# RWKV inverse on 64x64 pieces, with keys prepared at full height and decayed queries on GpSimd

## The chip, the cores and the metric

The kernel runs on one core of a Trainium2 chip. A core has five engines that run beside one another, each through its own queue in order: TensorE (PE in the profile, its weight loads PEld), VectorE (DVE), ScalarE (ACT), GpSimd (POOL) and SyncE (SP, which issues the transfers here). The metric is the device time of one execution, in microseconds (us), as the median of several runs.

## The reference, cut to what matters

The program is a backbone of two layers over 256 context tokens and 1,024 latent tokens, 1,024 wide. Layer 0 runs an RWKV-7 branch (8 heads of 64 columns) beside a Mamba-2 branch; layer 1 runs an mLSTM branch beside attention. Only the RWKV branch is touched. Per head and direction the reference scans the tokens with a 64x64 state S:

```python
kk = hs(k * p['k_k'])
kk = kk / jnp.maximum(jnp.sqrt(jnp.sum(kk * kk, -1, keepdims=True)), 1e-12)
k_dir = k[:, :, None] * (1.0 + (a - 1.0) * p['k_a'])
y, S_fin = rwkv7_bidir_scan(hs(r), hs(k_dir), hs(v), hs(decay), hs(a), kk, S0)
```

At each token the state is decayed per key column, loses what it holds along kk (weighted by a), and gains the outer product of value and key; the output is the state applied to r.

## The kernel before, in words

**The stage.** RWKV runs as a stage of its own in layer 0. The 512 columns make four column tiles (ct) of 128 partitions, two heads in each: head h lies on partitions H[h], 0 to 63 or 64 to 127. Tokens are cut into chunks of 64. A unit (`rwkv_unit`) takes NG = 2 chunks of both directions, that is NJ = 4 blocks j, for both heads; a column tile has 10 units, so there are 40. Two streams run side by side: stream 0 has column tiles 0 and 1, stream 1 has 2 and 3. In a stream the unit q+1 is prepared while the chain (`rwkv_chain`) of unit q carries the state, one step of the chain to two of the unit (`pace`). Beside them go, by `rwkv_stream`, the preparation of the next column tile (`rwkv_prep`) and the closing of the last (`rwkv_finish`), and at the start the output projection of the other branch (tile `oa`).

**What a unit does.** It loads r, k, kk and the low-rank inputs, and forms the gate a and the decay (lines 685 to 711). Lines 713 to 720 prepare: AR holds, for each block, the decayed kk (slot 0) and the decayed queries (slot 1), 128 partitions high. KB holds for each block the two keys divided by the decay, the removal key P*a and the gain key P*kd, in two slots whose order differs between the heads, so four half-height products write it. RZ holds the decayed queries of each head with zeros in the other head's rows. Then matmuls of KB against AR give all products of a chunk (line 727); they are masked into MN (line 730).

**The inverse.** Within a chunk the removals depend on one another, which is a triangular 64x64 system; its inverse is built by doubling in lines 740 to 780. MT and TT are 128x128 for each block: head 0's 64x64 in one corner, head 1's in the other, and zeros elsewhere (set once, lines 578 and 582). Line 752 makes the start, TT = MT times the mask m1. Then for b = 2 to 32 a matmul px (MT against Tm), a masked copy Xs, a matmul pz (TT against Xs) copied to Tm, and a matmul pt (Xs against TT) that ScalarE copies back to the two corners of TT (line 779). The helper `halves` issues each of these as eight matmuls, over blocks and heads. Each contracts over all 128 rows, takes one head's 64 columns, and writes that head's 64 partitions.

**The chain.** For each of the two chunks: pw, copied with a minus sign to w; pu, which is TT against w (line 817); pS, the new state; py, the output. In pw, pS and py the operands MN, KT and RZ hold both heads over all 128 rows.

**What sets the order.** The queues of this stage aren't written out by hand: a planner orders the instructions of each engine from their dependencies and its own estimates of time, and puts the semaphores. A matmul has no line of its own in the profile: all are recorded at line 212 of the helper `mm`, transposes at line 215, so they are told apart by their tiles (out<-moving,stationary). Tiles `rec` are those of the unit, `ch` those of the chain.

Of the kernel before, what the change touches and what calls it, by code (L numbers as in the profile page):

```python
# [8 lines left out]
F32 = mybir.dt.float32  # L9
# [3 lines left out]
ALU = mybir.AluOpType  # L13
# [11 lines left out]
NG = 2  # L25
# [22 lines left out]
def _masks():  # L48
    parts = []
    o = 0  # L50

    def put(name, a):
        nonlocal o
        a = np.asarray(a, np.float32).reshape(128, -1)
        _MK[name] = (o, a.shape[1])
        parts.append(a)
        o += a.shape[1]

    put("id", np.eye(128))
    put("ones", np.ones((128, 128)))  # L60
    r = np.arange(128)
    hh = (r[:, None] // 64 == r[None, :] // 64)
    put("bd1", hh)
    put("triu", r[:, None] <= r[None, :])
    put("slt", r[:, None] < r[None, :])
    for d in range(2):
        ok = (r[:, None] <= r[None, :]) if d == 0 else (r[:, None] >= r[None, :])
        put(f"mb{d}", np.where(ok, 0.0, -1e30))
    put("end", np.zeros((128, 0)))
    i = r % 64  # L70
    mp, m1, lv = [], [], {b: [] for b in (1, 2, 4, 8, 16, 32)}
    for d in range(2):
        bef = (i[:, None] < np.arange(64)[None]) if d == 0 else (i[:, None] > np.arange(64)[None])
        inc = bef | (i[:, None] == np.arange(64)[None])
        beffull = (i[:, None] < i[None, :]) if d == 0 else (i[:, None] > i[None, :])
        mp += [np.concatenate([bef, inc], 1)] * NG
        m1.append((hh & beffull & (i[:, None] // 2 == i[None] // 2)) | np.eye(128, dtype=bool))
        for b in lv:
            c = np.arange(64)[None]
            lv[b].append(~inc & (i[:, None] // (2 * b) == c // (2 * b)) & (i[:, None] // b != c // b) | (i[:, None] == c))  # L80
    put("mP", np.concatenate(mp, 1))
    put("m1", np.concatenate(m1, 1))
    put("id2", i[:, None] == np.arange(64)[None])
    for b in lv:
        put(f"l{b}", np.concatenate(lv[b], 1))
    return np.ascontiguousarray(np.concatenate(parts, 1))
# [64 lines left out]
class K:  # L151
# [401 lines left out]
    def rwkv_setup(s, rp):  # L553
        nc = s.nc
        s.rp = rp
        s.mk2 = rp.tile([128, MASKS.shape[1] - NMK], F32, name="mk2")
        s.load(s.mk2, s.I["masks"][:, NMK:])
        s.w2 = rp.tile([128, 512], F32, name="w2")
        s.a2 = rp.tile([128, 512], F32, name="a2")
        s.load(s.w2, s.I["w2"])  # L560
        s.load(s.a2, s.I["a2"])
        s.smask = rp.tile([128, 2, NG, 64], F32, name="smask")
        nc.vector.memset(s.smask, 1.0)
        for d in range(2):
            nc.vector.memset(s.smask[:, d, :, 63 * d:63 * d + 1], 0.0)
        s.rc = rp.tile([128, 28], F32, name="rc")
        nc.vector.tensor_scalar_mul(s.rc[:, 0:16], s.p("w0", 0, 16), 0.5)
        ka = s.p("k_a", 0, 4)
        nc.vector.tensor_scalar_mul(s.rc[:, 16:20], ka, 0.5)
        nc.vector.tensor_scalar(s.rc[:, 20:24], ka, -0.5, 1.0, ALU.mult, ALU.add)  # L570
        nc.vector.tensor_scalar(s.rc[:, 24:28], ka, -1.0, 2.0, ALU.mult, ALU.add)
        s.tt, s.wa, s.rz, s.mt = {}, {}, {}, {}
        for st in range(2):
            for i in range(2):
                s.tt[st, i] = rp.tile([128, 2 * NG, 128], F32, name=f"TT{st}{i}")
                s.wa[st, i] = rp.tile([128, 2, 2, 64 * NG], F32, name=f"wa{st}{i}")
                s.rz[st, i] = rp.tile([128, 2 * NG, 2, 64], F32, name=f"RZ{st}{i}")
                nc.gpsimd.memset(s.tt[st, i], 0.0)
                nc.gpsimd.memset(s.wa[st, i], 0.0)
                nc.gpsimd.memset(s.rz[st, i], 0.0)  # L580
            s.mt[st] = rp.tile([128, 2 * NG, 128], F32, name=f"MT{st}")
            nc.gpsimd.memset(s.mt[st], 0.0)
        s.RX = {}
        s.tn = [0, 0]
        s.kk_d = [s.dram("kkd", (128, NT)) for _ in range(4)]
        s.bv_d = [s.dram("bvd", (128, NT)) for _ in range(4)]
        s.vt_d = [s.dram("vtd", (128, 20, 64)) for _ in range(4)]
# [60 lines left out]
    def rwkv_unit(s, st, ct, gi):  # L648

        nc, rp = s.nc, s.rp  # L650
# [6 lines left out]
        H = [slice(0, 64), slice(64, 128)]  # L657

        def tl(nm, w, bufs=1):
            return rp.tile([128, NJ] + list(w), F32, tag=f"{nm}{st}", name=s.name(nm), bufs=bufs)  # L660
# [4 lines left out]
        def rec(*sh):  # L665
            return s.psum(f"rec{st}", (128, NJ) + sh)

        r, k, kk = tl("ur", [64]), tl("uk", [64]), tl("ukk", [64])
# [3 lines left out]
        TT, RZ, MT = s.tt[st, par], s.rz[st, par], s.mt[st]  # L672
# [15 lines left out]
        sg, a = tl("sg", [64]), tl("a", [64])  # L688
        for j, x in ((0, sg), (1, a)):
            for d in range(2):  # L690
                b = 8 * j + 4 * d + ct
                nc.scalar.activation(flat(x)[:, L * d:L * d + L], pp[:, j, d], AF.Tanh, bias=s.rc[:, b:b + 1], scale=0.5)
        yield
        kd = tl("kd", [64])
        nc.vector.tensor_scalar(sg, sg, 0.5, 0.5, ALU.mult, ALU.add)
        nc.vector.tensor_scalar(kd, a, s.rc[:, 16 + ct:17 + ct], s.rc[:, 20 + ct:21 + ct], ALU.mult, ALU.add)
        nc.vector.tensor_scalar(a, a, 0.5, 0.5, ALU.mult, ALU.add)
        P = tl("P", [64])
        for d in range(2):
            def v(x):  # L700
# [4 lines left out]
        E2 = tl("E2", [64], 2)  # L705
# [1 line left out]
        nc.scalar.activation(E2, P, AF.Exp, scale=-DEC)  # L707
        nc.scalar.activation(P, P, AF.Exp, scale=DEC)
        nc.scalar.activation(sg, sg, AF.Exp, scale=-DEC)
        nc.gpsimd.tensor_mul(a, kk, a)  # L710
        nc.gpsimd.tensor_mul(kd, kd, k)
        yield
        AR = tl("AR", [2, 64])
        nc.vector.tensor_mul(AR[:, :, 0], sg, kk)
        nc.vector.tensor_mul(AR[:, :, 1], E2, r)
        KB = tl("KB", [2, 64])
        for h in range(2):
            nc.vector.tensor_mul(KB[H[h], :, h], P[H[h]], a[H[h]])
            nc.vector.tensor_mul(KB[H[h], :, 1 - h], P[H[h]], kd[H[h]])
            nc.gpsimd.tensor_mul(RZ[H[h], :, h], E2[H[h]], r[H[h]])  # L720
        yield
        MN = tl("MN", [2, 2, 64], 2)
        mP = s.m("mP").rearrange("p (j a b) -> p j a b", a=2, b=64)
        pa = [rec(2, 64) for h in range(2)]
        for j in range(NJ):
            for h in range(2):
                s.mm(pa[h][:, j].rearrange("p a b -> p (a b)"), KB[H[h], j].rearrange("p a b -> p (a b)"),
                     AR[H[h], j].rearrange("p a b -> p (a b)"))
        for h in range(2):
            nc.vector.tensor_mul(MN[:, :, :, h], pa[h], mP)  # L730
# [8 lines left out]

        ident = s.m("id")  # L740
        for h in range(2):
            nc.vector.scalar_tensor_tensor(MT[H[h], :, H[h]], MN[H[h], :, 0, h], -1.0,
                                           ident[H[h], H[h]].unsqueeze(1).to_broadcast([64, NJ, 64]), ALU.mult, ALU.add)
        KT = tl("KT", [2, 64], 2)
        pk = [rec(64) for h in range(2)]
        for j in range(NJ):
            for h in range(2):
                s.tr(pk[h][:, j], KB[H[h], j].rearrange("p a b -> p (a b)"), ident[H[h], H[h]])
        for h in range(2):
            nc.scalar.copy(KT[:, :, h], pk[h])  # L750
            nc.scalar.copy(MN[H[h], :, 0, h], AR[H[h], :, 0])
# [3 lines left out]
        def halves(fn):  # L755
            for j in range(NJ):
                for h in range(2):
                    fn(j, H[h])

        Tm = tl("Tm", [64], 2)  # L760
        px = rec(64)
        halves(lambda j, Q: s.mm(px[Q, j], MT[:, j, Q], s.m("id2")))
        nc.vector.tensor_mul(dj(Tm), dj(px), bj("l1"))  # L763
        yield
        for b in (2, 4, 8, 16, 32):
            px = rec(64)
            halves(lambda j, Q: s.mm(px[Q, j], MT[:, j, Q], Tm[:, j]))
            Xs = tl("Xs", [64])
            nc.vector.tensor_mul(dj(Xs), dj(px), bj(f"l{b}"))
            yield  # L770
            if b < 32:
                pz = rec(64)
                halves(lambda j, Q: s.mm(pz[Q, j], TT[:, j, Q], Xs[:, j]))
                Tm = tl("Tm", [64], 2)
                nc.scalar.copy(Tm, pz)
            pt = rec(64)
            halves(lambda j, Q: s.mm(pt[Q, j], Xs[:, j], TT[:, j, Q]))
            for h in range(2):
                nc.scalar.copy(TT[H[h], :, H[h]], pt[H[h]])  # L779
            yield  # L780
        X["u", gi] = {"E2": E2, "MN": MN, "KT": KT, "SV": SV, "TT": TT, "RZ": RZ}

    def rwkv_chain(s, st, ct, gi):
        nc, rp = s.nc, s.rp
        X = s.RX[ct]
        H = [slice(0, 64), slice(64, 128)]
        U = X["u", gi]
        SV, TT, MN, KT, E2, RZ = (U[k] for k in ("SV", "TT", "MN", "KT", "E2", "RZ"))
# [11 lines left out]
        def ch():  # L800
            return s.psum(f"ch{st}", (128, 2, 64))

        E = E2.rearrange("p j l -> p (j l)")
        ident = s.m("id")
        for n in range(NG):
# [5 lines left out]
            w = rp.tile([128, 2, 64], F32, tag=f"w{st}", name=s.name("w"))  # L811
            nc.scalar.mul(w, pw, -1.0)
            yield
            pu = ch()
            for d, j in enumerate(js):
                for h in range(2):
                    s.mm(pu[H[h], d], TT[:, j, H[h]], w[:, d])
            nc.vector.tensor_copy(both(SV, n)[H[0], :, 1, 0], pu[H[0]])
            nc.scalar.copy(both(SV, n)[H[1], :, 1, 1], pu[H[1]])
            yield  # L820
# [1226 lines left out]
```

## Time and profile before

| | |
|---|---|
| median of 3 runs | 3814.51 us (3805.86 to 3820.41) |
| the profiled execution | 3798.59 us |
| its span, first to last instruction | 3796.8 us |
| busy: PE | 3400.6 us (90%) |
| busy: DVE | 2253.9 us (59%) |
| busy: ACT | 1575.3 us (41%) |
| busy: POOL | 1087.7 us (29%) |
| mean granted clock of TensorE | 0.934 |
| first and last matmul of the inverse (tile rec) | 978.7 and 1882.4 us |

How to read it: times of rows are busy times of one profiled execution. A matmul's end is modelled and matmuls overlap, so PE's busy time is more than what it needs; the time from start to start tells more. In a group row stand the line, engine, operation, out<-in by the program's names, partitions x elements, the count, then the sum of busy time, the mean of one in ns, and the idle time before with what ended it. "128*64" on a matmul means 128 rows by 64 columns of the array.

### The profile page before, as it was taken

The numbers are of one execution on the slowest core, as the hardware profiler recorded it, in microseconds if no ns is written. First come the engines' busy times: TensorE is split into PE (matmuls) and PEld (weight loads), VectorE is DVE, ScalarE is ACT, GpSimd is POOL, SyncE is SP. The second block draws the span as 40 slices with busy tenths as digits, with TensorE's granted clock in tenths as the row PEclk, the third lists the DMA queues.
The fourth block names the chain that finished last, engine by engine and source line by source line (L and its number), as shares of the span: only waits on it lengthen the run. The fifth ranks groups of instructions, "written<-read, shape, count | busy, mean of one in ns | idle before, by whom it ended". The sixth has DMA issues, their size and how long they took to land. (4 is left out here: it accounts for less than half of the span.)

```text
span 3796.8 us, 74389 instructions
## 1 busy us (share of the span) xinstructions
PE 3400.6 (90%) x29178; PEld 2723.1 (72%) x29178; DVE 2253.9 (59%) x4173; ACT 1575.3 (41%) x3419; POOL 1087.7 (29%) x1037
## 2 busy tenths in 40 slices
PE   7999998886898898789869899999999788999978
PEld 3687876673577777677757798788888566666757
DVE  3576587773566667677557705433444488677645
ACT  3232233333535656555533322322232225666751
POOL 0112266553322221121102212112222255444330
PEclk9999998997899988799879999999999899999989
DMA  6526454436543222221132322654554451000023
GB/s 237 180 75 199 138 173 149 156 124 182 153 124 99 63 69 65 82 56 47 32 111 100 124 91 85 190 180 138 161 160 147 146 157 54 23 23 22 19 81 111
DMA packets 394278, 429.65 MB, mean 113 GB/s; under 512 B 81376, under 2 KB 317760, under 8 KB 391368
## 3 DMA queue, kind: packets, MB, share of 16 engines
q1 hardware_dynamic: 393928, 424.90, 35.7%
q8 instruction: 230, 3.77, 0.4%
q14 instruction: 120, 0.98, 0.1%
HBM read 306.69 MB, written 118.05 MB: 112 GB/s over the span
## 5 line engine op out<-in xcount | busy, mean ns | idle before, releaser
L212 PE MATMUL mm<-hh,wh 128*128 128x512 f32 (+1 forms) x1640 | 634.8, 387 | 0.0
L212 PE MATMUL mm<-hh,wl 128*128 128x512 f32 (+1 forms) x1640 | 610.4, 372 | 0.9 <-POOL wl L359 0.9
L212 PE MATMUL mm<-hl,wh 128*128 128x512 f32 (+1 forms) x1640 | 610.6, 372 | 0.0
L359 POOL TENSOR_TENSOR wl<-wr,wh 128x1024 fp32r<-128x1024 f32 x99 | 248.3, 2512 | 543.1 <-ACT wh L358 520.9
L212 PEld LDWEIGHTS mm<-hh,wh 128*128 128x128 f32 x1640 | 315.0, 192 | 67.8 <-issue 12.7
L212 PEld LDWEIGHTS mm<-hl,wh 128*128 128x128 f32 x1640 | 314.6, 192 | 61.4 <-issue 10.6
L212 PEld LDWEIGHTS mm<-hh,wl 128*128 128x128 f32 x1640 | 313.9, 191 | 59.5 <-issue 3.4
L1792 POOL TENSOR_SCALAR aP<-aP,adn,one 128x1280 f32<-128x1280 f32 x128 | 191.9, 1499 | 283.5 <-DVE adn L1791 160.5
L212 PE MATMUL mm<-wh,hh 128*128 128x256 f32 x736 | 217.1, 295 | 0.0
L1785 DVE TENSOR_REDUCE amx<-sc 128x1 f32<-128x1024 f32 x128 | 156.1, 1219 | 101.6 <-PE sc L212 101.4
L212 PE MATMUL mm<-wl,hh 128*128 128x256 f32 x736 | 208.6, 283 | 3.4 <-POOL wl L359 2.5
L212 PE MATMUL mm<-wh,hl 128*128 128x256 f32 x736 | 208.2, 283 | 0.0
L215 PE MATMUL tp<-mk,aP 128*128 128x128 f32 x1280 | 181.9, 279 | 4.7 <-ACT aPT L1800 4.7
L1800 ACT COPY aPT<-tp 128x512 f32<-128x512 f32 x256 | 145.4, 587 | 83.6 <-PE tp L215 81.9
L215 PEld LDWEIGHTS tp<-mk,aP 128*128 128x128 f32 x1280 | 143.5, 142 | 35.7 <-issue 21.2
L212 PE MATMUL pv<-aPT,aV 128*64 128x256 f32 x1280 | 168.8, 395 | 0.0
L358 ACT CAST wh<-wr 128x1024 fp32r<-128x1024 f32 x99 | 103.2, 1045 | 152.7 <-PE mm L212 123.9
L779 ACT COPY TT<-rec 64x256 f32<-64x256 f32 x400 | 146.4, 366 | 37.6 <-PE rec L212 19.4
L212 PE MATMUL sc<-akT,aqs 128*128 128x512 f32 x512 | 153.9, 423 | 1.7 <-DVE aqs L1770 1.1
L1073 POOL TENSOR_SCALAR sel<-mk,mdfd,mdt 128x128 f32<-128x128 f32 x160 | 128.7, 818 | 76.7 <-DVE E L1097 57.7
L212 PE MATMUL rec<-Tm,MT 128*64 128x64 f32 x3200 | 138.4, 229 | 13.5 <-DVE Tm L763 6.6
L212 PE MATMUL oa<-wh,yh 128*128 128x512 f32 x288 | 127.3, 442 | 22.3 <-DVE o L1224 10.9
(425 smaller groups left out, 8136.8 us busy)
## 6 DMA issues: line engine op xcount, KB each, us to landing
wr<-in_wcd SPq DMA_DIRECT2D x60, 512.0 KB, 5.7
adaw<-in_ada SPq DMA_DIRECT2D x48, 512.0 KB, 5.2
R<-rowd SPq DMA_DIRECT2D x20, 1024.0 KB, 5.3
wr<-in_wab SPq DMA_DIRECT2D x38, 512.0 KB, 4.0
yr<-y SPq DMA_DIRECT2D x36, 512.0 KB, 4.2
xt<-xtok SPq DMA_DIRECT2D x20, 512.0 KB, 5.3
SV<-vtd SPq DMA_DIRECT2D x320, 32.0 KB, 2.2
lva<-lv SPq DMA_DIRECT2D x19, 514.0 KB, 5.0
```

Source lines behind the costliest of these rows:

```text
L212: return s.nc.tensor.matmul(out, lhsT, rhs, start=start, stop=stop)
L215: return s.nc.tensor.transpose(out, in_, ident)
L358: nc.scalar.copy(hi, raw)
L359: nc.gpsimd.tensor_sub(lo, raw, hi.bitcast(F32))
L779: nc.scalar.copy(TT[H[h], :, H[h]], pt[H[h]])
L1073: nc.gpsimd.tensor_scalar(sel[:, h], s.m("slt"), s.dfd[:, o:o + 1], dtb[:, h:h + 1], ALU.mult, ALU.add)
L1785: nc.vector.tensor_reduce(mx[:, 1:2], ps, AX.X, ALU.max)
L1792: nc.gpsimd.tensor_scalar(P, P, dn[:, 3:4], s.one, ALU.mult, ALU.mult)
L1800: copy(out, pp.rearrange("p (a b) q -> p a (b q)", a=out.shape[1]))
```

## The change

It does four things. First, MT and TT shrink to 128 x 64 for each block: head h's 64x64 piece lies on its own partitions, without the zero corners. So the matmuls px, pz, pt and pu contract over the 64 rows of one head alone; the masks m1 shrink likewise; the six memsets of MT and TT go; and ScalarE writes pt back with one copy over 128 partitions instead of two over 64. Second, KB gets three slots: the removal key of both heads lies in slot 1, written by one full-height product, and the gain key in slot 2 for head 0 and slot 0 for head 1; a helper kb(j, h) picks the two slots that a matmul reads. Third, the gate step becomes (a + 1) * kk in one VectorE instruction (it was 0.5 * a + 0.5 on VectorE and then a product with kk on GpSimd), and the factor 0.5 goes into the key product. Fourth, both products of AR move from VectorE to GpSimd, the queries' first.

```diff
-        m1.append((hh & beffull & (i[:, None] // 2 == i[None] // 2)) | np.eye(128, dtype=bool))
+        c = np.arange(64)[None]
+        m1.append(bef & (i[:, None] // 2 == c // 2) | (i[:, None] == c))
...
-                s.tt[st, i] = rp.tile([128, 2 * NG, 128], F32, name=f"TT{st}{i}")
+                s.tt[st, i] = rp.tile([128, 2 * NG, 64], F32, name=f"TT{st}{i}")
...
-                nc.gpsimd.memset(s.tt[st, i], 0.0)
...
-            s.mt[st] = rp.tile([128, 2 * NG, 128], F32, name=f"MT{st}")
-            nc.gpsimd.memset(s.mt[st], 0.0)
+            s.mt[st] = rp.tile([128, 2 * NG, 64], F32, name=f"MT{st}")
...
-        nc.vector.tensor_scalar(a, a, 0.5, 0.5, ALU.mult, ALU.add)
+        nc.vector.scalar_tensor_tensor(a, a, 1.0, kk, ALU.add, ALU.mult)
...
-        nc.gpsimd.tensor_mul(a, kk, a)
         nc.gpsimd.tensor_mul(kd, kd, k)
         yield
         AR = tl("AR", [2, 64])
-        nc.vector.tensor_mul(AR[:, :, 0], sg, kk)
-        nc.vector.tensor_mul(AR[:, :, 1], E2, r)
-        KB = tl("KB", [2, 64])
+        KB = tl("KB", [3, 64])
+        nc.gpsimd.tensor_mul(AR[:, :, 1], E2, r)
+        nc.vector.scalar_tensor_tensor(KB[:, :, 1], P, 0.5, a, ALU.mult, ALU.mult)
+        nc.gpsimd.tensor_mul(AR[:, :, 0], sg, kk)
         for h in range(2):
-            nc.vector.tensor_mul(KB[H[h], :, h], P[H[h]], a[H[h]])
-            nc.vector.tensor_mul(KB[H[h], :, 1 - h], P[H[h]], kd[H[h]])
+            nc.vector.tensor_mul(KB[H[h], :, 2 - 2 * h], P[H[h]], kd[H[h]])
+        for h in range(2):
             nc.gpsimd.tensor_mul(RZ[H[h], :, h], E2[H[h]], r[H[h]])
+
+        def kb(j, h):
+
+            return KB[H[h], j, 1 - h:3 - h].rearrange("p a b -> p (a b)")
...
-                s.mm(pa[h][:, j].rearrange("p a b -> p (a b)"), KB[H[h], j].rearrange("p a b -> p (a b)"),
+                s.mm(pa[h][:, j].rearrange("p a b -> p (a b)"), kb(j, h),
...
-            nc.vector.scalar_tensor_tensor(MT[H[h], :, H[h]], MN[H[h], :, 0, h], -1.0,
+            nc.vector.scalar_tensor_tensor(MT[H[h]], MN[H[h], :, 0, h], -1.0,
...
-        halves(lambda j, Q: s.mm(px[Q, j], MT[:, j, Q], s.m("id2")))
+        halves(lambda j, Q: s.mm(px[Q, j], MT[Q, j], s.m("id2")[Q]))
...
-            halves(lambda j, Q: s.mm(px[Q, j], MT[:, j, Q], Tm[:, j]))
+            halves(lambda j, Q: s.mm(px[Q, j], MT[Q, j], Tm[Q, j]))
...
-                halves(lambda j, Q: s.mm(pz[Q, j], TT[:, j, Q], Xs[:, j]))
+                halves(lambda j, Q: s.mm(pz[Q, j], TT[Q, j], Xs[Q, j]))
...
-            halves(lambda j, Q: s.mm(pt[Q, j], Xs[:, j], TT[:, j, Q]))
-            for h in range(2):
-                nc.scalar.copy(TT[H[h], :, H[h]], pt[H[h]])
+            halves(lambda j, Q: s.mm(pt[Q, j], Xs[Q, j], TT[Q, j]))
+            nc.scalar.copy(TT, pt)
...
-                    s.mm(pu[H[h], d], TT[:, j, H[h]], w[:, d])
+                    s.mm(pu[H[h], d], TT[H[h], j], w[H[h], d])
```

More of the change, by code (lines that the diff above doesn't have):

```diff
@@ L74, in _masks @@
         inc = bef | (i[:, None] == np.arange(64)[None])
-        beffull = (i[:, None] < i[None, :]) if d == 0 else (i[:, None] > i[None, :])
         mp += [np.concatenate([bef, inc], 1)] * NG
-        m1.append((hh & beffull & (i[:, None] // 2 == i[None] // 2)) | np.eye(128, dtype=bool))
+        c = np.arange(64)[None]
+        m1.append(bef & (i[:, None] // 2 == c // 2) | (i[:, None] == c))
         for b in lv:
-            c = np.arange(64)[None]
             lv[b].append(~inc & (i[:, None] // (2 * b) == c // (2 * b)) & (i[:, None] // b != c // b) | (i[:, None] == c))
@@ L747, in rwkv_unit @@
             for h in range(2):
-                s.tr(pk[h][:, j], KB[H[h], j].rearrange("p a b -> p (a b)"), ident[H[h], H[h]])
+                s.tr(pk[h][:, j], kb(j, h), ident[H[h], H[h]])
         for h in range(2):
```

## The prediction

> **What bounds the kernel now.** I read the page first, for the whole and for the clock; then the windows, to find the RWKV stage and to cut it into stretches; then the waits inside it; then the groups, for prices; and last the order of PE's instructions.
>
> ```profile
> span 3796.8 us, 74389 instructions
> PEclk9999998997899988799879999999999899999989
> 966.00:1250.00 284.00, 252.91 (x3526) 197.99 (x3527) 175.89 (x328) 136.32 (x342) 80.69 (x77) 0.90 0.40 119
> 1250.00:1640.00 390.00, 337.70 (x6233) 280.62 (x6234) 261.68 (x591) 232.31 (x623) 73.69 (x98) 0.84 0.25 70
> 1640.00:1850.00 210.00, 194.27 (x4679) 171.36 (x4676) 148.13 (x358) 127.73 (x394) 37.80 (x48) 1.00 0.17 43
> 1850.00:1895.00 45.00, 33.13 (x620) 27.41 (x615) 22.65 (x47) 21.10 (x54) 4.38 (x6) 0.79 0.13 37
> ```
>
> The last four rows are the windows view: stretch, length, busy time of PE, PE's weight loads, DVE, ACT and POOL, then granted clock. Everything that the diff touches lies in these 929 us of the 3796.8. Until about 1250 the projection of the other branch runs beside it; until 1640 there is side work (preparing the next heads, finishing old ones); from 1640 to 1850 the two streams run alone. There PE is busy 194 of 210 us, DVE 148, ACT 128. A busy PE overstates, since matmuls overlap. So I look at what engines wait for.
>
> ```profile
> ACT Tm L775 <- PE rec L212: 101.2, 88, 6.3
> DVE Xs L769 <- PE rec L212: 78.4, 63, 3.4
> PE rec L212 <- DVE KB L719: 16.5, 17, 3.1
> ```
>
> These are waits over 966 to 1895: total, times, longest. ACT and DVE wait for PE's inverse matmuls far more (101 and 78 us) than PE waits for them; the one visible wait of PE on a line of the change is for the keys (line 719), 16.5 us. The stage is a mixture, with PE the engine that is waited for, most of all after 1640.
>
> **What is taken from DVE and ACT.**
>
> ```profile
> L718 DVE TENSOR_TENSOR KB<-P,a 64x256 f32<-64x256 f32 x79 | 44.1, 559 | 10.7 <-POOL a L710 6.5 <-ACT P L708 3.1
> L719 DVE TENSOR_TENSOR KB<-P,kd 64x256 f32<-64x256 f32 x79 | 39.1, 495 | 1.2 <-POOL kd L711 1.1
> L752 DVE TENSOR_TENSOR TT<-MT,mk 128x512 f32<-128x512 f32 x40 | 27.3, 682 | 0.2
> L715 DVE TENSOR_TENSOR AR<-E,ur 128x256 f32<-128x256 f32 x39 | 25.0, 641 | 5.4 <-ACT E L707 5.1
> L714 DVE TENSOR_TENSOR AR<-sg,ukk 128x256 f32<-128x256 f32 x39 | 24.9, 637 | 2.6 <-ACT sg L709 2.5
> L697 DVE TENSOR_SCALAR a<-a 128x256 f32<-128x256 f32 x39 | 24.1, 617 | 0.2
> L763 DVE TENSOR_TENSOR Tm<-rec,mk 128x256 f32<-128x256 f32 x40 | 16.8, 420 | 17.6 <-PE rec L212 17.1
> L619 DVE SCALAR_TENSOR_TENSOR sm<-sm,pf,r 128x256 f32<-128x256 f32 x15 | 7.3, 483 | 7.8 <-POOL sm L618 6.8 <-DMA x<-in_x 0.9
> L779 ACT COPY TT<-rec 64x256 f32<-64x256 f32 x400 | 146.4, 366 | 37.6 <-PE rec L212 19.4 <-PE ch L212 0.7
> L775 ACT COPY Tm<-rec 128x256 f32<-128x256 f32 x160 | 59.5, 372 | 103.1 <-PE rec L212 101.2
> L710 POOL TENSOR_TENSOR a<-ukk,a 128x256 f32<-128x256 f32 x39 | 29.6, 758 | 30.8 <-DVE a L697 18.6 <-DMA uk<-urk 3.7 <-DMA wa<-urk 3.7
> L720 POOL TENSOR_TENSOR RZ<-E,ur 64x256 f32<-64x256 f32 x78 | 64.0, 820 | 91.1 <-PE ch L212 75.4 <-ACT TT L779 8.3 <-ACT E L707 2.3
> L578 POOL MEMSET TT<- 128x512 f32 x4 | 2.1, 523 | 0.0
> ```
>
> There are 40 units. Per unit DVE loses both AR products (0.641 + 0.637 = 1.28 us). Of the four half-height key products (2 x 0.559 + 2 x 0.495 = 2.11) two stay (0.99) and one full-height scalar_tensor_tensor comes, 0.48 by line 619: saved 0.64. The a step becomes the same form, 0.617 to 0.483: 0.13. The first mask product halves its width, 0.682 to the 0.420 of a 128x256 product: 0.26. That is 2.31 us, or 92 us of DVE's 608 in the stage. ACT writes TT with one 128x256 copy (0.372) where it made two (2 x 0.366), five times a unit: 1.8 us, 72 us in all. A copy takes as long for 64 partitions as for 128, which is why joining the halves pays.
>
> GpSimd loses the product a (0.758) and gains two like it: net +0.76 us per unit, 30 us in all, on an engine busy 197 of 929. They sit in its in-order queue behind kd and ahead of the two RZ products (0.820 each). RZ is needed only late in the chain, so I cost this at nothing; if RZ became late, the y matmuls would wait by up to 1.5 us a unit. The new AR wait is for PE: its first matmuls need both AR products, about 1.5 us after the exponentials, where DVE needed 3.4 for AR and keys together (1.28 + 2.11). The six memsets that go (0.523 each) run before the stage, on an idle queue; the narrower mask load and memory are free too.
>
> How much of 4.1 us per unit (2.31 + 1.8) is on the path? Bounds: 0 (all under PE) and 164 us. PE visibly waits 16.5 us for keys; the copies save queueing on ACT, whose big idle entries are PE. I take a quarter, 1.0 us per unit: **-40 us**, with -10 to -80 as ends.
>
> **What is given to PE.** Number and width of matmuls are unchanged. But px, pz, pt and pu, which used 128 rows by 64 columns (128*64), become 64 rows by 64 columns. The chain's other matmuls (pw, pS, py) stay at 128*64, because their operands hold both heads over all rows.
>
> ```profile
> 984.08 0.69 PE L212 MATMUL rec<-Xs,TT 128*64 128x64 f32 x16
> 984.59 0.64 PE L212 MATMUL rec<-TT,Xs 128*64 128x64 f32 x16
> 985.16 0.70 PE L212 MATMUL mm<-al,a 64*128 64x256 f32 x2
> 971.73 0.59 PE L212 MATMUL mm<-sm,mk 128*128 128x256 f32 x2
> 972.25 0.46 PE L215 MATMUL rec<-mk,KB 64*128 64x64 f32 x4
> 972.64 0.50 PE L212 MATMUL oa<-wh,yl 128*128 128x512 f32 x1
> ```
>
> This is the timeline of PE alone. Sixteen 64-wide matmuls take 0.51 us from their start to the next group (0.032 each) when the next has the same shape of array, though the weights change with every one. Four transposes of 64 rows, between two neighbours of 128 rows, take 0.39 where four at 0.032 would be 0.13: 0.26 more for one change in and one out, and only the row count differs here. So a change of shape costs PE 0.10 to 0.15 us; I take **0.12**. No row shows 64*64 beside 128*64, so the price could be 0 there. I take 0.12 because the nearest rows, those just above, change the rows alone and pay.
>
> The Trainium skill, in TensorEngine Tiling (Array Packing), section Key Properties, says that changing the tiling mode, not just the tile, drains the engine, and its list has 64x64 and 128x64 as two configurations. By that rule the sum is +25 us as below, without it -40; the rows above agree for other pairs of shapes, and no run yet shows this pair.
>
> ```profile
> 1708.24 0.22 PE L212 MATMUL ch<-SV,MN 128*64 128x64 f32 x1
> 1708.27 0.22 PE L212 MATMUL rec<-Tm,MT 128*64 128x64 f32 x1
> 1708.30 0.22 PE L212 MATMUL ch<-SV,RZ 128*64 128x64 f32 x1
> 1708.33 0.22 PE L212 MATMUL rec<-Tm,MT 128*64 128x64 f32 x1
> 1708.36 0.22 PE L212 MATMUL ch<-SV,RZ 128*64 128x64 f32 x1
> L212 PE MATMUL rec<-Tm,MT x3200: 222/222/369, 978.7 to 1878.6; 128*64 128x64 f32 x189
> ```
>
> Here lies the trouble. The inverse (rec) and the chain (ch) alternate one by one, 0.03 us apart, at no cost because both are 128*64. After the change each such step is a change of shape. The last row gives the first and last of the 3,200 matmuls of one of these groups; over this stretch I counted neighbours of unlike shape through PE's records: 485 now, 1,483 if the order stays and the four kinds become 64*64. Of the 998 new ones 150 lie before 1250, 347 up to 1640, 470 up to 1850, 31 behind; 880 stand where PE now goes on within 0.06 us, so they hide under no wait.
>
> 998 x 0.12 = 120 us of PE. On the path by stretch: 1640 to 1850 has 4,679 matmuls x 0.032 = 150 us, plus 119 changes now x 0.12 = 14, so PE needs 164 of 210; with 56 more it needs 220, more than the stretch lasts. Full overlap would give +10, none +56; I take +36. From 1250 to 1640 it needs 6,233 x 0.032 + 197 x 0.12 = 223 of 390, so there is room; I take half of 42, +21. Before 1250 a third of 18, +6; behind 1850 +2. Sum **+65**, ends 0 and +150.
>
> **Sum:** +65 - 40 = +25 us. The profiled execution took 3798.59 (span 3796.8 and 1.8 around it), 16 below the median of 3814.51; from 3798.6 I get 3823.6, and against the median shown **3840 us**. Within 0.5% (19 us) a measurement of this kernel can hardly be told from no change.
>
> **Rivals.**
>
> *The shape change is free (or the planner stops alternating).* Then only the -40 stands: 3775, down to 3735 if half of the relief is on the path. For it: no row shows this pair. Against it: every other pair in the trace pays. Fewest changes with the order regrouped: six 128-row groups a unit, in and out, 12 x 40 = 480 against 998, 58 us of PE, about +31 on the path, so -9: near 3805. It ends on the faster side once the price per change falls under about 0.07 us (40 / 65 x 0.12). Chance 0.22.
>
> *The clock comes up.*
>
> ```profile
> 1408.00:1412.00 4.00, 3.37 (x52) 2.24 (x48) 2.64 (x9) 3.71 (x12) 1.19 (x1) 1.00 0.20 48
> 1412.00:1416.00 4.00, 1.10 (x17) 0.91 (x16) 1.48 (x5) 1.74 (x7) 2.31 (x4) 0.86 0.22 50
> 1416.00:1420.00 4.00, 4.00 (x22) 3.01 (x21) 3.94 (x11) 0.42 (x1) 2.54 (x4) 0.50 0.28 65
> ```
>
> When both streams prepare at once, PE thins to 1.10 busy of 4 us and the clock falls from 1.00 to 0.50; 1250 to 1640 averages 0.84. With the keys ready sooner these holes may close. A clock of 1.00 would give PE 16% more in those 390 us, at most 62 us; I put half of it at 31, which with the +25 gives -6: 3808. Against it: the loads that open the holes stay. Chance 0.15.
>
> *The clock goes down.* In 1640 to 1850 the clock never fell. Gaps of 0.12 us at 470 places, and half of the rows idle, may read as a PE less active. At 0.84, as in the stretch before, 210 us become 250: +40 on top of +25, 3880. It decides if thinning in that stretch reaches the level of 1412. The Trainium skill, TensorE: Matmul & The Clock Gate, section Part 1, ties the half rate to an idle window of some 3.4 us; by that rule alone this rival would not happen, as no such window is idle, but the row at 1412 shows a fall with PE at 1.10 of 4 us, and the row decides. Chance 0.15.
>
> **Chances and range.** My forecast has 0.48, with a range of its own from 3815 to 3880 (half to all of the price on the path). Faster by over 0.5%: nearly all of the first rival, a third of the second, a little of the forecast, 0.30. Slower by over 0.5%: some six tenths of the forecast and the third rival, 0.45. The rest, 0.25, within. The range of 8 in 10 takes in the first rival's middle and the third: 3755 to 3905.
>
> **What would show it.** In the profile after: PE's groups of the inverse and of ch<-w,TT read 64*64; in the timeline of a stretch like 1708 an alternating step from rec to ch takes 0.13 to 0.15 us instead of 0.03; copies of TT number 200 at 0.37 and are 128x256; DVE's sum in the stage falls by about 90 us, ACT's by 70, POOL's rises by 30; PE's wait for keys shrinks under 10 us. I am wrong if the step stays near 0.03, if rec and ch no longer alternate, or if the stretch of the two streams alone gets shorter than 210 us.

## The result, and the profile after

The kernel after takes 3828.74 us (median of 20 runs, 3821.75 to 3838.69), the kernel before 3809.31 (20 runs beside them, 3797.21 to 3820.59). The ratio is 1.0054, 95% interval 1.0043 to 1.0065: slower by some 20 us. The forecast was 3840, slower by 25.

The profiled execution after took 3834.97 us, 6 above its median; that of before lay 11 below its own. So of the 36.4 us between the two traces some 17 are the spread between executions, and the parts below are sized by timed runs, not by this pair of traces. The page of after first, its span and clock:

```profile
span 3833.2 us, 74118 instructions
PEclk9999998997798989789969999999999898999989
```

The windows of after, in the stretches of the prediction (stretch, length, busy time of PE, weight loads, DVE, ACT, POOL, then clock, DMA share, GB/s):

```profile
966.00:1250.00 284.00, 257.97 (x3482) 201.17 (x3482) 154.44 (x286) 118.45 (x289) 86.00 (x84) 0.87 0.40 118
1250.00:1640.00 390.00, 340.29 (x6161) 278.02 (x6161) 250.46 (x545) 206.09 (x547) 91.48 (x116) 0.86 0.25 70
1640.00:1850.00 210.00, 198.39 (x4174) 171.72 (x4170) 113.53 (x284) 92.87 (x287) 41.46 (x53) 0.93 0.16 41
1850.00:1926.00 76.00, 62.98 (x1235) 52.80 (x1234) 39.23 (x90) 33.60 (x93) 10.99 (x14) 0.86 0.11 30
```

Read the counts: up to 1640 the kernel after has issued nearly as many matmuls as before (9,643 against 9,759), but from 1640 to 1850 it issues 4,174 where before issued 4,679, at a clock of 0.93 where before had 1.00. The inverse ends at 1913 instead of 1882. By this reading alone nearly all is lost while the two streams run alone; the experiments show that this is a balance of several parts and misleads.

Rows out of the groups of after, over 960 to 1930 (sum, mean in ns, idle before):

```profile
L780 ACT COPY TT<-rec 128x256 f32<-128x256 f32 x200 | 74.5, 373 | 52.1 <-PE rec L211 36.3 <-PE ch L211 0.4
L715 DVE TENSOR_TENSOR KB<-P,kd 64x256 f32<-64x256 f32 x80 | 56.7, 709 | 2.6 <-POOL kd L707 1.5
L711 POOL TENSOR_TENSOR AR<-E,ur 128x256 f32<-128x256 f32 x40 | 31.3, 784 | 135.6 <-ACT E L704 132.0 <-PE rec L211 2.3 <-PE ch L211 1.1
L713 POOL TENSOR_TENSOR AR<-sg,ukk 128x256 f32<-128x256 f32 x40 | 31.2, 779 | 25.5 <-issue 9.0 <-ACT sg L706 5.2 <-DMA wa<-urk 3.5
L694 DVE SCALAR_TENSOR_TENSOR a<-a,ukk 128x256 f32<-128x256 f32 x40 | 29.1, 727 | 0.2
L712 DVE SCALAR_TENSOR_TENSOR KB<-P,a 128x256 f32<-128x256 f32 x40 | 23.1, 578 | 7.6 <-ACT P L705 7.2
L754 DVE TENSOR_TENSOR TT<-MT,mk 128x256 f32<-128x256 f32 x40 | 18.8, 469 | 0.4
```

ACT's copies came out as forecast (200 at 0.373 us). VectorE's did not: the gain key, the same 64x256 product as before, went from 495 to 709 ns, and the gate step takes 727 where it was to take 483. Rows out of the waits of after, over 960 to 1930 (total, times, longest):

```profile
ACT Tm L777 <- PE rec L211: 140.0, 121, 7.1
DVE Xs L771 <- PE rec L211: 107.1, 88, 3.3
PE rec L211 <- POOL AR L713: 37.5, 17, 4.9
PE rec L211 <- DVE KB L715: 7.8, 7, 3.3
```

PE's wait for the inputs of a unit's first matmuls has grown from 16.5 us to 45.3, most of it for GpSimd's AR, and ACT and DVE wait longer for PE. The order of PE's work, from the timeline of after (start, length, group):

```profile
1742.87 0.68 PE L211 MATMUL rec<-Tm,MT 64*64 64x64 f32 x16
1743.53 0.34 PE L211 MATMUL ch<-SV,MN 128*64 128x64 f32 x4
...
1757.41 0.63 PE L211 MATMUL rec<-Xs,TT 64*64 64x64 f32 x16
1757.88 0.63 PE L211 MATMUL rec<-TT,Xs 64*64 64x64 f32 x16
```

Sixteen inverse matmuls take 0.47 us up to the next group when that has the same shape, and 0.66 when it has not. The 0.66 also holds a part of the change ahead of that group, so these two rows alone give too high a price. Over all of PE's records of the stage, eight steps from matmul to matmul take 0.38 us with one change among them and 0.23 without (medians), and sixteen steps 0.615 and 0.467: 0.15 us for one change. Within one shape the eight steps take 0.23 us before the change too, so the matmuls on 64 rows are not slower by themselves. And the inverse and the chain no longer alternate one by one: they come in runs of up to 16. Counted through PE's records of the stage there are 482 changes between 64*64 and 128*64 (70, 200, 165 and 47 in the four stretches); the step itself mostly takes 0.148 to 0.152 us from start to start.

### The profile page after: what moved, and what is told of

The parts are those of the page before. It is cut to its first block, busy times and chain, and to the rows that moved or that the text cites. A ratio compares the mean times of both kernels' runs of the same rounds, so it can differ in the third digit from the quotient of the medians.

```text
span 3833.2 us, 74118 instructions
## 1 busy us (share of the span) xinstructions
PE 3442.4 (90%) x29178; PEld 2751.3 (72%) x29178; DVE 2197.4 (57%) x4053; ACT 1510.3 (39%) x3219; POOL 1118.5 (29%) x1071
## 5 line engine op out<-in xcount | busy, mean ns | idle before, releaser
L771 DVE TENSOR_TENSOR Xs<-rec,mk 128x256 f32<-128x256 f32 x200 | 84.3, 423 | 110.5 <-PE rec L211 107.1
L211 PEld LDWEIGHTS mm<-wl,hh 128*128 128x128 f32 x736 | 141.8, 193 | 3.2 <-POOL wl L358 2.0
```

The lines of the kernel that those rows point to most:

```text
L211: return s.nc.tensor.matmul(out, lhsT, rhs, start=start, stop=stop)
```

## The experiments

Theory A: the changes of shape are the loss, the new preparation of keys and queries a gain. Theory B: GpSimd's AR products are the loss, and the inverse on pieces is neutral. All twelve kernels were timed beside the kernel before; "us" is the ratio less one, times 3808 (the median of before in these runs). The last columns are from the one trace of each kernel, by counting PE's records: when 7,392 of the 10,560 matmuls of tile rec have started (as many as 28 of the 40 units have), when the last has, and the clock from 1640 to 1850.

| | kernel | ratio (95%) | us | 28th unit | last | clock |
|---|---|---|---|---|---|---|
| - | before | 1 | 0 | 1674 | 1882 | 1.00 |
| - | after | 1.0054 (1.0043 to 1.0065) | +21 | 1683 | 1913 | 0.93 |
| 1 | inverse alone | 1.0088 (1.0071 to 1.0105) | +34 | 1693 | 1924 | 0.92 |
| 2 | preparation alone | 1.0009 (0.9997 to 1.0020) | +3 | 1677 | 1893 | 0.94 |
| 3 | after, AR on VectorE | 1.0002 (0.9992 to 1.0012) | +1 | 1664 | 1886 | 1.00 |
| 4 | after, pu at 128 rows | 1.0074 (1.0059 to 1.0090) | +28 | 1691 | 1922 | 0.94 |
| 5 | keys alone, AR on VectorE | 0.9913 (0.9896 to 0.9929) | -33 | 1651 | 1858 | 0.99 |
| 6 | as 3, two copies of TT | 1.0002 (0.9983 to 1.0022) | +1 | 1674 | 1896 | 1.00 |
| 7 | as 3, queries on GpSimd | 1.0027 (1.0014 to 1.0041) | +10 | 1670 | 1897 | 0.96 |
| 8 | before, vt shares a buffer | 1.0004 (0.9992 to 1.0016) | +2 | 1679 | 1887 | 1.00 |
| 9 | as 5, pu on 64 rows | 0.9929 (0.9906 to 0.9952) | -27 | 1662 | 1871 | 1.00 |
| 10 | as 5, old gate step | 0.9954 (0.9935 to 0.9972) | -18 | 1672 | 1878 | 1.00 |
| 11 | before, new gate step | 0.9965 (0.9946 to 0.9983) | -13 | 1671 | 1879 | 1.00 |
| 12 | as 5, GpSimd loaded | 1.0006 (0.9992 to 1.0020) | +2 | 1671 | 1892 | 0.97 |

**1, the inverse alone.** The diff's lines for MT, TT, m1, px, pz, pt, pu and the one copy, with KB and AR as before.

> Only the inverse and the product pu work on 64x64 pieces, with one copy of TT on ScalarE; keys and queries are prepared as before the change. Theory A (the loss is the 482 changes of array shape between 64*64 and 128*64 at 0.15 us; the new preparation is a gain): slower than the kernel before by 20 to 40 us, ratio 1.005 to 1.010, and PE's wait for the keys stays near 16 us. Theory B (the loss is PE's new wait for the AR products on GpSimd, which also lets the clock fall; the inverse on pieces costs nothing on balance): ratio 0.995 to 1.000.

Measured 3839.86 us, 34 above before, with 492 changes between the two shapes. Theory A's size; B's neutral inverse is out. One sign of A failed, though: PE's wait for the keys is 28 us here (23.8 and 4.2 on the two lines of the keys) and not near 16, so the 34 us may hold more than the changes themselves. And that one part costs more than the whole change says that the other part must gain.

**2, the preparation alone.**

```diff
+        nc.vector.scalar_tensor_tensor(a, a, 1.0, kk, ALU.add, ALU.mult)
...
+        nc.gpsimd.tensor_mul(AR[:, :, 1], E2, r)
+        nc.vector.scalar_tensor_tensor(KB[:, :, 1], P, 0.5, a, ALU.mult, ALU.mult)
+        nc.gpsimd.tensor_mul(AR[:, :, 0], sg, kk)
```

> Only the preparation is changed (keys at full height in three slots, a in one instruction, both AR products on GpSimd); the inverse stays on 128 rows. One side tile shares a buffer with another, to make room for the third slot. Theory A: no new changes of shape, so faster by 10 to 25 us, ratio 0.993 to 0.997. Theory B: PE waits about 35 to 40 us for AR on GpSimd, ratio 1.003 to 1.007.

Measured 3811.82, a gain of nothing. PE waits as theory B said:

```profile
PE rec L212 <- POOL AR L716: 39.3, 21, 4.0
```

Neither theory holds by itself: A's gain is not there, B's loss is not there either.

**3, the kernel after with AR back on VectorE.**

```diff
-        nc.gpsimd.tensor_mul(AR[:, :, 1], E2, r)
+        nc.vector.tensor_mul(AR[:, :, 1], E2, r)
...
-        nc.gpsimd.tensor_mul(AR[:, :, 0], sg, kk)
+        nc.vector.tensor_mul(AR[:, :, 0], sg, kk)
```

> The kernel after, with both AR products back on VectorE. Theory A: the changes of shape stay, and VectorE gets 1.3 us per unit more, so as slow as the kernel after or slower, ratio 1.005 to 1.010. Theory B: PE's wait for line 713 (37.5 us) goes and a wait for the keys of about 15 us comes back, half-rate intervals of the clock after 1640 us go, ratio 0.995 to 1.000.

Measured 3809.46, at the edge of theory B's range and far from A's: moving two products back to the busier engine gains 20 us against the kernel after. PE's wait for these inputs is 18 us again, and the clock from 1640 to 1850 is 1.00:

```profile
PE rec L211 <- DVE KB L715: 18.1, 14, 3.7
```

With 486 changes still in it the kernel is no slower than before, so something in the new keys must pay for them.

**4, pu back at 128 rows.** The last level of pt goes by two copies into a 128-wide tile TF with zero corners, and pu reads that.

```diff
-                    s.mm(pu[H[h], d], TT[H[h], j], w[H[h], d])
+                    s.mm(pu[H[h], d], TT[:, j, H[h]], w[:, d])
```

> The kernel after, but the last level of the inverse is written by two copies into a separate 128-wide tile with zero corners, so that pu contracts over 128 rows again and the chain has one shape; ScalarE has one more copy per unit (15 us in all). The second buffer of TT is given up and one side tile shares a buffer. Changes between 64*64 and 128*64 fall from 482 to some 320. Theory A: 160 changes fewer at 0.15 us, 24 us of PE, about half of it on the path: faster than the kernel after by 8 to 15 us, ratio to the kernel before 1.001 to 1.004. Theory B: no gain, ratio 1.005 to 1.008.

A miss: the planner made 521 changes, not 320, since it grouped the work otherwise. Measured 3836.63. It tests nothing that was meant; it has more changes and is slower, but it also lost a buffer of TT and gained a copy.

**5, the keys alone, with AR on VectorE**, on the inverse of 128 rows: experiment 2 with the swap of experiment 3.

> The kernel before with the new keys alone (three slots, a in one instruction), both AR products on VectorE, the inverse on 128 rows; one side tile shares a buffer. Theory A (changes of shape cost, the new keys gain): it has the gain of the keys without the price, so faster than the kernel before by 8 to 20 us, ratio 0.995 to 0.998, and no half-rate spell from 1640 to 1850 us. If the parts simply added, it would be before minus the 32 us between the first and the third experiment, ratio 0.992. Theory N (what was seen is the planner's order, which any edit shuffles by some 10 us): ratio 0.998 to 1.002.

Measured 3774.77 (3769.25 to 3782.31), 33 us under before: below the range that theory A gave, and just where the parts add. It is the fastest kernel of this study, faster than before and after. But the gain does not show in PE's wait for the keys, which is 23.2 us here (the row stands under experiment 12) and was 16.5 before. It shows in the stretch from 1250 to 1640, where PE starts 6,636 matmuls, 403 more than before, at a clock of 0.88 where before had 0.84:

```profile
1250.00:1640.00 390.00, 336.22 (x6636) 281.31 (x6638) 265.98 (x601) 243.77 (x659) 65.08 (x82) 0.88 0.26 72
```

**6, two copies of TT.** The kernel of experiment 3 with

```diff
-            nc.scalar.copy(TT, pt)
+            for h in range(2):
+                nc.scalar.copy(TT[H[h]], pt[H[h]])
```

> The third experiment (the kernel after with AR on VectorE), but each level's result goes back to TT by two half-height copies as before the change, so ScalarE has 200 copies (73 us) more; against the fifth experiment only the shape of the matmuls differs. Theory A with the copies worth something: slower than the third by 5 to 15 us, ratio to before 1.002 to 1.005, and slower than the fifth by 14 to 30 us. If ScalarE is off the path: as the third, ratio 0.999 to 1.001.

Measured 3807.32, as experiment 3: the 73 us that ACT was relieved of are worth nothing that can be seen (interval of some 7 us each way). Experiments 5 and 6 differ by the shape of the inverse's matmuls (and a first mask product half as wide): 34 us, with 470 changes in 6 and none in 5.

**7, half of AR on GpSimd.** The kernel after with kk's product back on VectorE and the queries' left on GpSimd.

> The kernel after with the decayed kk back on VectorE and only the decayed queries on GpSimd. Theory B (GpSimd's two products in a row are late at each unit's start): PE's wait falls from 37 us to about 20 to 28, half-rate spells after 1640 us mostly go, ratio to before 1.000 to 1.003. Theory A alone (the AR products' place does not matter): ratio 1.004 to 1.007.

Measured 3821.13, in theory B's range: 10 us over experiment 3 for one product, where two cost 20. But the wait is not the one that B names. PE waits 28.1 us, for VectorE's key and not for GpSimd's product:

```profile
PE rec L211 <- DVE KB L715: 28.1, 23, 4.2
```

**8, a control.** One side tile in another's buffer, as in 2, 4, 5, 9, 10 and 12.

> The kernel before, with one tile of the side work (vt) in the buffer of another (a1) and nothing else: a control for the second, fourth and fifth experiments, and a measure of what a neutral edit does to the planner's order. If these orders are worth little: ratio 0.999 to 1.001. If the planner's order moves the time by 10 us by itself: outside 0.9975 to 1.0025.

Measured 3810.71, ratio 1.0004. The shared buffer costs nothing that shows, and whatever this neutral edit did to the planner's order moved the time by no more than that.

**9, a small dose of shape changes.** Experiment 5 with `s.mm(pu[H[h], d], TT[H[h], j, H[h]], w[H[h], d])`.

> The fifth experiment (new keys, AR on VectorE, inverse on 128 rows) with pu alone on 64x64 pieces, taken out of the corners of the 128-wide TT: a small dose of changes of shape and nothing else changed. At most 160 changes between 64*64 and 128*64 (80 groups of pu, in and out), against 470 to 490 of the full inverse, which cost 32 us: theory A, price by count: 5 to 11 us above the fifth, ratio to the kernel before 0.9925 to 0.9945. If the price of the full inverse lies elsewhere (in the 64-row matmuls themselves or in the copies): as the fifth, 0.991.

Measured 3787.96, with 126 changes. The ratio lies 0.0016 above that of experiment 5: 6 us, in the forecast span; the medians lie 13 us apart, and the intervals of the two overlap. It agrees with a price by count within this spread and doesn't prove it.

**10 and 11, the two halves of the keys.** In 10 the gate step is as before (0.5 a + 0.5 on VectorE, the product with kk on GpSimd) and only the slots are new; in 11 only the gate step is new.

> The fifth experiment with the gate step as before the change (0.5 a + 0.5 on VectorE, then the product with kk on GpSimd): the three slots and the full-height key alone. If the gain of 33 us is VectorE's time (0.64 of the 0.77 us per unit come from the slots): ratio 0.992 to 0.994. If it is the step over GpSimd that the one instruction saves: 0.997 to 1.000.

> The kernel before with the gate step alone changed ((a + 1) * kk in one instruction on VectorE, the factor 0.5 in the key products, four half-height products in two slots). If the gain is VectorE's time (0.13 of 0.77 us per unit): ratio 0.998 to 1.000. If it is the step over GpSimd: 0.992 to 0.995. The two parts should add up to 33 us.

Measured 3793.12 and 3795.42: by the ratios -18 and -13, together -31 of the -33 (by the medians -14 and -12). Both lie between the ranges given, so neither VectorE's time alone nor the step over GpSimd alone carries the gain. Experiment 11 is the telling one. It takes 30 us of work from GpSimd and hardly any from VectorE (the new step takes 763 ns, the old 623), and it gains 13 us. What it is worth must come from GpSimd: from the load on it, or from the step over it, for which VectorE's removal key waited 6.5 us before. This run does not tell which.

**12, the load on GpSimd by itself.** Experiment 5, in which GpSimd also computes both AR products, into the tile k (uk in the profile), which nobody reads any more. PE uses VectorE's.

```diff
+        nc.gpsimd.tensor_mul(k, E2, r)
+        nc.gpsimd.tensor_mul(k, sg, kk)
         for h in range(2):
             nc.gpsimd.tensor_mul(RZ[H[h], :, h], E2[H[h]], r[H[h]])
```

> The fifth experiment with both AR products on VectorE, and GpSimd computing the same two products as well, into a tile that nobody reads: GpSimd's queue and its memory traffic are as in the kernel after, but PE waits for VectorE's copies only. If the 37 us between the second and the fifth experiment are GpSimd's lateness: as the fifth, ratio 0.990 to 0.993. If they are the load on GpSimd's queue (kd, RZ later) or its traffic slowing VectorE (the key product went from 495 to 709 ns): 0.997 to 1.002.

Measured 3811.93, ratio 1.0006: 37 us lost against experiment 5 by two products (34.0 and 32.7 us of GpSimd's time) that no one waits for. That is as much as between 5 and 2, where PE does wait for them. Late AR products aren't needed to explain the loss; the load is enough. The groups of VectorE and the wait of PE, in experiment 5 (two views):

```profile
L718 DVE TENSOR_TENSOR KB<-P,kd 64x256 f32<-64x256 f32 x80 | 41.2, 515 | 1.7 <-POOL kd L710 0.6
L774 DVE TENSOR_TENSOR Xs<-rec,mk 128x256 f32<-128x256 f32 x200 | 83.2, 422 | 75.6 <-PE rec L212 73.0
```

```profile
PE rec L212 <- DVE KB L718: 23.2, 20, 3.7
```

and in experiment 12:

```profile
L718 DVE TENSOR_TENSOR KB<-P,kd 64x256 f32<-64x256 f32 x80 | 59.1, 739 | 1.7 <-POOL kd L710 0.6
L776 DVE TENSOR_TENSOR Xs<-rec,mk 128x256 f32<-128x256 f32 x200 | 83.3, 422 | 75.3 <-PE rec L212 72.5
```

```profile
PE rec L212 <- DVE KB L718: 41.2, 30, 4.0
```

The key product, with both inputs in the on-chip memory (SBUF), goes from 515 to 739 ns; Xs, one of whose inputs is PE's output, stays at 422. That the longer queue makes kd late is not the reason: VectorE waited 0.6 us for kd in both, and PE has no wait for RZ in either. Taken one by one, the key product takes 0.42 us (median) where no GpSimd instruction overlaps it, 57 of 80 times in experiment 5 and 25 of 80 in 12; where one does, it takes 0.84 and 0.93. How this comes about stands in the timeline of experiment 12, VectorE first, then GpSimd:

```profile
1684.73 0.95 DVE L715 SCALAR_TENSOR_TENSOR KB<-P,a 128x256 f32<-128x256 f32 x1
1685.60 0.94 DVE L716 TENSOR_TENSOR AR<-sg,ukk 128x256 f32<-128x256 f32 x1
...
1690.69 2.26 DVE L749 SCALAR_TENSOR_TENSOR MT<-MN,mk 64x256 f32<-64x256 f32 x2
...
1696.12 0.43 DVE L715 SCALAR_TENSOR_TENSOR KB<-P,a 128x256 f32<-128x256 f32 x1
...
1702.07 0.86 DVE L749 SCALAR_TENSOR_TENSOR MT<-MN,mk 64x256 f32<-64x256 f32 x2
```

```profile
1684.49 0.91 POOL L722 TENSOR_TENSOR RZ<-E,ur 64x256 f32<-64x256 f32 x1
1685.36 0.90 POOL L720 TENSOR_TENSOR uk<-sg,ukk 128x256 f32<-128x256 f32 x1
...
1690.39 0.72 POOL L722 TENSOR_TENSOR RZ<-E,ur 64x256 f32<-64x256 f32 x1
1691.08 0.72 POOL L719 TENSOR_TENSOR uk<-E,ur 128x256 f32<-128x256 f32 x1
1691.88 0.79 POOL L722 TENSOR_TENSOR RZ<-E,ur 64x256 f32<-64x256 f32 x1
```

The removal key takes 0.43 us at 1696, when GpSimd rests, and 0.95 at 1684.73, when GpSimd has begun RZ at 1684.49: it ends 0.3 us after RZ does. Both MT steps, for which PE's px waits, take 0.86 us alone and 2.26 beside three GpSimd products. VectorE waits for GpSimd instead of working beside it; GpSimd's own rows change less (0.72 to 0.91 here).

The Trainium skill, SBUF — State Buffer, section Who interferes with whom, says that a VectorE instruction with two inputs in SBUF contends with a GpSimd instruction that reads SBUF. These rows agree.

## Why the prediction was right, and where it was not

The direction and the rough price of a change of shape were right, but that the sum came out (+25 forecast, +20 measured) is luck: the changes of shape and the keys came 31 and 23 us below their terms, the copies and AR 17.5 and 32.5 above, and these errors cancelled. Each term against what the runs gave:

| term | forecast | measured | from |
|---|---|---|---|
| changes of shape | +65 | +34 | 1 over before; 3 over 5; 6 over 5 |
| copies of TT on ACT | -17.5 | 0 | 6 against 3 |
| AR off VectorE, on GpSimd | -12.5 | +20 | after over 3 |
| keys, gate step, mask product | -10 | -33 | 5 under before; 3 under 1 |
| sum | +25 | +21 | |

(The forecast's -40 is split here by its own us per unit: 1.8 for the copies, 1.28 for AR, 1.03 for the rest, of 4.11. The measured mask product lies in the first row.) The parts add well: the new keys give 33 us on the old inverse and 33 on the new one. Only the inverse and GpSimd's load together cost less, 17 us for the inverse between 2 and after instead of 34.

**The price of a change of shape** was right in kind and somewhat low: 0.12 us forecast, 0.15 measured (0.38 us for eight steps against 0.23). So the first rival, that it is free, fell.

**The count of 998** was the step that failed in this term: it took the order of before as fixed. The planner grouped the two streams' work by shape and left 482, as the rival's side case had it (480). That rec and ch no longer alternate was one of the forecast's own signs of being wrong, and it came. 482 x 0.15 = 72 us of PE, of which 34 show, 0.47; the forecast had 120 and 0.54.

**"I take a quarter"** failed as a single share for all the relief. ACT's share is nothing, and I had the reason in hand: its big idle entries were waits for PE. The keys gain 33 us, twice the 16.5 us of PE's wait for them (line 719) and all of the 31 us (0.77 x 40) that VectorE was to save on the keys and the gate step. They stand between the exponentials and a unit's first matmuls, but the wait did not shrink in experiment 5, so that row gave neither the size nor the place of the gain.

**"So I cost this at nothing"**, said of GpSimd's two added products, is the step that failed outright, and with it the forecast that PE's wait for keys would shrink under 10 us (45.3 measured, 37.5 of it on AR) and that VectorE would lose 90 us. Summed over the stage, by the windows of the prediction and those above, VectorE went from 608 to 558 us, ACT from 517 to 451 and POOL from 197 to 230. So ACT fell by 66 and POOL rose by 33, near the 70 and 30 forecast; VectorE fell by 51 instead of 90, mostly because what runs on it is slower beside GpSimd: the gain key takes 17 us more than before, the gate step 10 more than priced. Beside a GpSimd instruction ran 21 of the 80 gain keys before and 51 after. I had priced GpSimd's work by its own queue and asked only who waits for it. It had to be priced by what it does to VectorE as well.

**The clock.** The rival that it comes up between 1250 and 1640 fell for the change as it stands (0.84 before, 0.86 after), but for the keys alone it is nearer to what happened (0.88 in experiment 5). The rival that it goes down from 1640 to 1850 came true in part: 0.93, at most 15 us of the 210 (0.07 x 210), not the 40 that it was priced at. From 1640 to 1850 it fell in all kernels with more work on GpSimd and in experiment 1, and stayed at 1.00 in 3 and 6, which have as many changes of shape: gaps of 0.15 us at the changes do not lower it by themselves. In the windows of after one can watch it go, behind a stretch in which PE is thin because it waits 2.32 us for AR:

```profile
1706.00:1710.00 4.00, 1.68 (x36) 1.21 (x36) 3.59 (x7) 3.09 (x11) 3.39 (x4) 1.00 0.25 73
1710.00:1714.00 4.00, 4.00 (x50) 3.42 (x51) 3.75 (x10) 0.70 (x2) 1.57 (x2) 0.58 0.36 94
```

So a late input can cost PE more than the wait: the work behind it runs at a lower clock. How much of the time that is can be estimated from the clock and span of every timed run: the span times (1 - mean granted clock) is a ceiling of what the clock took, as it counts PE as the bound everywhere. Its medians are some 260 us before, 257 after, 271 in experiment 1, 263 in 2, 240 in 3, 234 in 5, 232 in 6 and 253 in 12. By this estimate up to 26 of the 33 us that the keys gain are clock, up to 17 of the 20 that AR on GpSimd costs (3 to after), and up to 20 of the 37 between 5 and 12; but at most 6 of the 34 between 5 and 3 and none between 5 and 6, so the changes of shape cost time at the full clock too. No run holds the clock still, so these shares are not shown.

**Where the loss seemed to lie.** Between the traces of before and after the gap opens mostly behind 1640. The table of experiments shows parts that largely cancel ahead of it: the keys bring unit 28 forward by 23 us (5), the new inverse takes 13 to 23 back (3 and 6 against 5), and GpSimd's load 19 more (after against 3). From unit 28 to the last the gain of the keys is almost nil (207 us in 5, 208 before), so there the two losses stand bare: 222 in 3 and 6, 230 after.

**Open.** Of the 37 us that GpSimd's load costs in experiment 12, PE's longer wait for the keys shows 18; slower MT steps and the lower clock are there to be seen, but no run sizes them apart. How the keys gain 33 us while PE's wait for them grows is not shown beyond the clock. Nor do 2 and 12 separate how late AR is on GpSimd from what VectorE saves by not making it: the two may offset each other. And the planner chose its order anew in each kernel; only one neutral edit was tried (2 us). Against mere chance of order speaks that the parts come out alike on different kernels (the keys 33 us twice, and 31 in halves).

## What to carry to other kernels

Before moving an elementwise product to a GpSimd that looks idle, look at which VectorE instructions run at that moment, those with two SBUF inputs above all, and whether PE waits for them: here a third to over a half of each microsecond given to GpSimd was lost (37 us for 67 in experiment 12, 20 for 62 between 3 and after). A change of the matmul's array shape is a price per alternation (0.15 us here), so count the alternations that the scheduler will leave, not those in the old order; and a saving is worth neither its busy time (73 us of ACT's copies gave nothing) nor the wait that it seems to stand in (33 us of the keys against a wait of 16.5): a run with each part alone settles it far better than a share applied to the sum. When parts of a change pull in different directions, keep the good one: the keys alone run at 0.9913 of the time before.

## What the runs showed of the hardware that I had not expected

- GpSimd holds VectorE up on products of two SBUF inputs: 0.43 us alone and 0.95 beside GpSimd for the same instruction, while Xs, which reads PE's output, stayed at 422 or 423 ns. The old gate step, with one SBUF input, is held up too: 0.29 us alone and 0.76 beside GpSimd (medians of 9 and 31 in the trace of before).
- A change between 64*64 and 128*64 takes 0.148 to 0.152 us for the step, where steps of 0.007 and 0.052 alternate within one shape, and the second pair behind it is spaced wider too (0.100 instead of 0.052 us): 0.15 us more in all. The Trainium skill, TensorEngine Tiling (Array Packing), section Key Properties, says that a change of mode drains the engine; the trace agrees as far as a change costs time, and gives the price here.
- A copy of 128x256 from PE's output on ACT takes 373 ns and one of 64x256 366, and still halving their number was worth nothing here.
